# Conditioning rows loaded into the activations' places, a later place for two steps of the first layer's mixers, and another order in the first and last head of the convolution

## The chip, the cores and the metric

The kernel runs on one core of a Trainium2 chip. The metric is the device time of one execution in microseconds (us), and the median of several executions is shown. A core has the engines TensorE (PE, matrix products and transposes), VectorE (DVE), ScalarE (ACT), GpSimd (POOL) and SyncE (SP). Here SP issues the transfers between memory and the core's buffers, one after the other in the order of its queue.

## The reference

A network of two layers works on 1280 tokens (256 of context, then 1024) of width 1024. Each sub-layer is a norm, a modulation by conditioning vectors, a mixer or SwiGLU, and a gated residual.

```
mod = silu(c) @ ada_w + ada_b                    # six vectors for each layer
h   = rmsnorm(x) * (1 + scale) + shift
# layer 0: 4 heads of a bidirectional mLSTM (chunks), and 32 groups of a bidirectional S5:
s_t = a * s_(t-1) + B u_t       (complex)         # the scan
y   = gelu(C s + d * u); b = (y @ wg) glu         # "glu"
x   = x + gate * (concat(norm(mlstm) * sigmoid(o), b) @ w_out)
# layer 1: q, k, v = silu(conv3x3(h @ w_in)), 8 heads of a gated delta rule, both directions
S_t = a_t (I - b_t k_t k_t^T) S_(t-1) + b_t k_t v_t^T;  o_t = S_t^T q_t
x   = x + gate * swiglu(...)                      # after the mixer of each layer
```

## The kernel before

Activations lie with features on the 128 partitions and tokens along the row, in three chunks of 256, 512 and 512 tokens (`CHUNKS`). A dense product splits both operands into a high and a low part and runs three matmuls for each of 8 slices (L124 to L126): `pd` takes 24 matmuls for 128 output features of one chunk, and that is the piece by which the program counts. Each weight block arrives as `w_raw` and is split by ACT (`w_hi`) and POOL (`w_lo`).

The work is written as generators that yield after each piece. `merge`, `take` and `chain` weave them, and the numbers at the head of the file say how many pieces of one go between those of another. PE's order is fixed by that (`in_pe_order`). The other engines are ordered by the framework's scheduler, which looks at a model of the time; marks such as `high_priority` and `issue_after` bind it.

**Entry** (`entry`, `load_x`, `cond_steps`). The tokens come as ten loads `x_raw` of 512 KB (two of context, eight of x), and are transposed to the activations by PE (`x_pt`). Their sums of squares go through a scratch row (`junk`). Two of the six vectors of layer 0, units (0, 0) and (0, 1), are needed for the first norm: their 8 MB come as sixteen `a_raw` loads of 512 KB. `x_raw` and `a_raw` share one ring of three buffers (`self.araw`). PE multiplies the rows with the vectors (`a_ps`), the result is copied to `a_sb`, transposed (`a_pt`), and the norm (`nb_ps`, then tiles `hh` and `hl`, high and low part of the activation) follows. Meanwhile DVE works out the poles of the S5 part (`s5_poles`).

**Layer 0 up to the mixers** (`layer0`). The projection `mlstm_project` has 48 pieces (16 blocks of weights by three chunks). `NI` of them stand in the chain that is merged with `s5_in_matrices` (DVE makes `s_w`, PE transposes it to `s_pb`), `NP` with the products `s_ps` that feed the scan, `NQ` with the matrices of the way out (`s_pk`), `NR` with `mlstm_gates` (`g_pt`), and the rest with the conditioning of the other four vectors. The scan itself runs on DVE, L1080 to L1083, four operations for a step, on the tile `bst`.

**Mixers.** `mlstm_outputs` goes through 12 groups (four heads, each in groups of 4, 4 and 2 chunks of tokens). For each group there are weights (`s_ps`, `e_ps`), heads (`z_ps`; `hsum` is normed by `nv` and `rstd`), and `mlstm_finish` some groups later (`y_pt` transposes `hsum`). The next head's states (`k_pt` and `v_pt` transpose `kT` and `vT`, DVE scales to `kd`, products `c_ps`) are woven in. `N1` of its pieces come alone, then `N2` pieces beside the 16 pieces of `s5_outputs` (`s_py`), then `N3` beside `M2` of `s5_glu`. `s5_outputs` first exchanges two halves of the scan's states by three transfers, each of which needs the one before:

```
with self.tc.issue_after(self.last_load):
    nc.sync.dma_start(out=sw, in_=a)      # L1095 sw_dr<-bst
    nc.sync.dma_start(out=a, in_=b)       # L1096 bst<-bst
    nc.sync.dma_start(out=b, in_=sw)      # L1097 bst<-sw_dr
```

`last_load` is the load of `vT` that was written last in the program (L565). `vT` has one buffer.

**Convolution of layer 1** (`gdn_project`, once for each of 8 heads). The three blocks of k, q and v are projected (`pd`), convolved on DVE (`cv_acc`) and put through a tanh (`d_fT`, `d_qT`). Side work is pulled between the matmuls of a `pd` at the places that the last argument of `conv_block` names, (3, 5) by default. The side work is `gdn_keys`: it transposes k and q to tokens (`tt_ps`), from the sums makes factors (`ei`, on ACT), transposes them (`d_pr`), DVE copies and subtracts (`rows`), and `d_pE` spreads the rows by matmuls. `K0`, `K1`, `Y1`, `Y2`, `L1`, `L2` are numbers of empty yields ahead of these steps. Heads 0 and 7 lay keys and queries in other places than heads 1 to 5, and heads 6 and 7 have no gate block of their own. `set_side` empties the old side work before it puts new work there.

Of the kernel before, what the change touches and what calls it, by code (L numbers as in the profile page):

```python
# [6 lines left out]
F32 = mybir.dt.float32  # L7
# [3 lines left out]
AF = mybir.ActivationFunctionType  # L11
# [16 lines left out]
HP = 400  # L28
Y1, Y2 = 6, 2
K0, K1, K2 = 4, 7, 3  # L30
R0, R1, R2, R3 = 3,1,1,2
F1, F2 = 20,8
L1, L2 = 4,2
F3, F4 = 18, 12
G1, G2, G3 = 2, 2, 14
N1, N2, N3, M2 = 40, 45, 68, 12
W1, W2, NI, NJ, NP, NK, NQ, NR = 1, 2, 2, 2, 4, 2, 10, 8

# [4 lines left out]
class Kernel:  # L43
# [137 lines left out]

    def cond_steps(self, i, m, kk):

# [4 lines left out]
        for k0 in range(0, KB, kk):  # L188
            raw = self.araw.tile([P, kk, D], F32, name="a_raw", tag="a_raw")
            src = w[k0 * P:(k0 + kk) * P, m * D:(m + 1) * D]  # L190
# [6 lines left out]
        sb = self.small.tile([P, 256], F32, name="a_sb", bufs=1)  # L197
        nc.vector.tensor_copy(sb, ps[:, :256])
        yield
# [13 lines left out]

    def cond_many(self, units, kk):
        for i, m in units:
            yield from self.cond_steps(i, m, kk)

# [111 lines left out]
    def load_x(self, hs):  # L329
# [3 lines left out]
        self.ssq = self.const.tile([P, NCH], F32, name="ssq0")  # L333
        junk = hs[2][1].rearrange("p k t -> p (k t)")[:, :D]
        for ci, (t0, n) in enumerate(CHUNKS):
            xt = self.xp.tile([P, KB, n], F32, name=f"x{ci}")
            self.x.append(xt)
            src = self.ins["ctx"][0] if ci == 0 else self.ins["x"][0]
            r0 = 0 if ci == 0 else t0 - NCTX
            for j in range(n // P):  # L340
                raw = self.araw.tile([P, D], F32, name="x_raw", tag="a_raw")
# [99 lines left out]
    def mlstm_gates(self, gk):  # L441
# [81 lines left out]
        self.negm = n1, n2  # L523
        yield
        mt = gp.tile(S, F32, name="g_mt")
        for c0 in range(0, NCH, 8):
# [47 lines left out]
    def mlstm_states(self, h, t, dp, wp):  # L574

        nc = self.nc
        kT, vT = t["kT"], t["vT"]
        vx = t["vx"] = dp.tile([P, NCH, 130], F32, name="vx")
        nc.gpsimd.memset(vx[:, :, 128:130], 1.0)
        kd = [wp.tile([P, NCH, P], F32, name=f"kd{r}") for r in range(2)]  # L580
        for c0, k in ((0, 4), (6, 4), (4, 2)):
# [10 lines left out]
            yield  # L592
        cs = t["cs"] = [dp.tile([P, NCH, 130], F32, name=f"cs{r}") for r in range(2)]
        for i in range(NCH - 1):
# [39 lines left out]
    def mlstm_heads(self, g, t, u, sp):  # L634
# [3 lines left out]
        qT, vx, cs = t["qT"], t["vx"], t["cs"]  # L638
        hsum = u["h"] = sp.tile([P, 4, P], F32, name="hsum", bufs=3)[:, :k]
        zs = [sp.tile([P, 4, 130], F32, name=f"z{r}") for r in range(2)]  # L640
# [25 lines left out]
        ss = sp.tile([P, 4], F32, name="hss")[:, :k]  # L666
        sq = sp.tile([P, P], F32, name="hsq")
        for c in range(k):
            nc.scalar.activation(out=sq, in_=hsum[:, c], func=AF.Square, accum_out=ss[:, c:c + 1])
        rstd = self.norm_rstd(ss, k, 1.0 / P)  # L670
# [17 lines left out]
    def mlstm_outputs(self, dp, wp, sp):  # L688
# [6 lines left out]
        n = len(self.GROUPS)  # L695
        for i in range(n + 3):
            parts = []
# [8 lines left out]
            yield from self.merge(parts)  # L706
            if i > 2:
                g = self.GROUPS[i - 3]
                yield from self.mlstm_finish(g, ts[g[0]], us[i - 3])
            if i < n and i % 3 == 0 and g[0] < 4:  # L710
# [17 lines left out]
    def emit(self, *streams):  # L728

        for _ in self.merge(streams):  # L730
            pass
# [399 lines left out]
    def entry(self, hs, mp, keep, st):  # L1131
# [11 lines left out]
        def emit(gen, n=1000):  # L1143
            for _ in self.take(gen, n):
                pass

        x = self.load_x(hs)
        with ExitStack() as s1:
            cp = self.pool("cp", 1, st=s1)
            self.cond_vectors(cp)  # L1150
            poles = self.s5_poles(keep)
            next(poles)
            emit(x, 2)
            cond = self.cond_many([(0, 0), (0, 1)], 1)
            emit(cond, 2)
            emit(poles)
            emit(cond, 2)
            self.cond_columns(cp)
            emit(self.merge([(cond, 16), (self.take(x, 4), 4)]))
        u_in = self.s5_inputs(hs, mp, self.pool("wu", 1, st=st))  # L1160
        with self.tc.issue_after(self.last_load):
            emit(u_in, 1)
        norm(0)
        norm(1)
# [227 lines left out]
    def layer0(self):  # L1392
# [6 lines left out]
        with ExitStack() as s0:  # L1399
# [4 lines left out]
            self.s5k = self.pool("s5q", 1, st=sk)  # L1404
            hs = [self.acts(ci) for ci in range(3)]
            with ExitStack() as s1:
# [18 lines left out]
            sk.close()  # L1425
            self.emit((self.take(proj, NR), NR), (self.mlstm_gates(mg), 9))
            self.conv_taps()
# [321 lines left out]
    def gdn_project(self, hs, h, tp, qp, kp, bp):  # L1749
# [3 lines left out]
        def start():  # L1753
            self.set_side(self.gdn_keys(h, kqv, kp, qp))
            self.pull()
        kT = tp.tile([P, T], F32, name="d_fT", bufs=3)
        self.conv_block(hs, D + h * P, 8 + h, kT, True, qp, (2, 3, 5, 6) if last else (3, 5))
        kqv[0] = kT
        self.nc.sync.dma_start(out=self.k_dr[h], in_=kT)
        qT = tp.tile([P, NLAT], F32, name="d_qT", bufs=2)  # L1760
        if last:
            start()
        self.conv_block(hs, h * P, h, qT, False, qp)
        kqv[1] = qT
# [15 lines left out]
    def gdn_keys(self, h, kqv, pool, qp):  # L1780

        nc = self.nc
        kT = kqv[0]
        if h == 7:
            for _ in range(L1):
                yield
        NQ = NCH + self.LCH
# [43 lines left out]
        ej = e3[:, 0]  # L1831
        for _ in range(K1 if together else Y1):
            yield
# [566 lines left out]
```

## Time and profile before

| what | before |
|---|---|
| median of 3 executions | 3572.6 us (3568.52 to 3575.85) |
| profiled execution | 3570.8 us |
| its span, first to last instruction | 3568.8 us |
| mean granted clock of PE | 0.967 of full |
| PE busy | 3341.3 us (94%), 18518 instructions |
| DVE busy | 1863.7 us (52%) |
| ACT busy | 1006.6 us (28%) |
| POOL busy | 971.9 us (27%) |

The span is what the trace covers, and the profiled execution has 2.0 us around it. A share over the whole span says little here, since the stages have different limits. Stages of the trace are: entry 0 to 130 us, layer 0 up to the end of the scan 481, mixers to 680, the rest of layer 0 and its SwiGLU to 1844, convolution to 2411, and the recurrence with the rest of layer 1 to 3569.

### The profile page before, as it was taken

The numbers are of one execution on the slowest core, as the hardware profiler recorded it, in microseconds if no ns is written. First come the engines' busy times: TensorE is split into PE (matmuls) and PEld (weight loads), VectorE is DVE, ScalarE is ACT, GpSimd is POOL, SyncE is SP. The second block draws the span as 40 slices with busy tenths as digits, with TensorE's granted clock in tenths as the row PEclk, the third lists the DMA queues.
The fourth block names the chain that finished last, engine by engine and source line by source line (L and its number), as shares of the span: only waits on it lengthen the run. The fifth ranks groups of instructions, "written<-read, shape, count | busy, mean of one in ns | idle before, by whom it ended". The sixth has DMA issues, their size and how long they took to land. (4 is left out here: it accounts for less than half of the span.)

```text
span 3568.8 us, 48262 instructions
## 1 busy us (share of the span) xinstructions
PE 3341.3 (94%) x18518; PEld 2796.5 (78%) x18527; DVE 1863.7 (52%) x4024; ACT 1006.6 (28%) x2409; POOL 971.9 (27%) x843
## 2 busy tenths in 40 slices
PE   5998979899999999999988999888999999999999
PEld 3787768788888888888777877668897788888888
DVE  6749977624433333333467777776654432323234
ACT  3221125422111111111245545543444211111112
POOL 1011123241111111111342382753334122222223
PEclk6999989999999999999999999899999999999999
DMA  7454676331222121121123334356553011111111
GB/s 235 112 172 128 211 197 192 107 127 36 77 83 66 60 83 60 59 71 42 54 69 97 117 119 125 119 139 204 170 167 111 18 54 45 53 45 54 42 53 65
DMA packets 396187, 360.29 MB, mean 101 GB/s; under 512 B 104123, under 2 KB 329115, under 8 KB 395446
## 3 DMA queue, kind: packets, MB, share of 16 engines
q1 hardware_dynamic: 395958, 357.22, 32.4%
q8 instruction: 146, 2.39, 0.3%
q14 instruction: 83, 0.68, 0.1%
HBM read 258.92 MB, written 96.75 MB: 100 GB/s over the span
## 5 line engine op out<-in xcount | busy, mean ns | idle before, releaser
L124 PE MATMUL pd<-hh,w_hi 128*128 128x512 f32 (+1 forms) x3064 | 1158.2, 378 | 3.0 <-ACT hh L289 2.0
L126 PE MATMUL pd<-hh,w_lo 128*128 128x512 f32 (+1 forms) x3064 | 1134.6, 371 | 5.6 <-POOL w_lo L118 5.2
L125 PE MATMUL pd<-hl,w_hi 128*128 128x512 f32 (+1 forms) x3064 | 1137.5, 371 | 2.4 <-DVE hl L281 2.2
L118 POOL TENSOR_TENSOR w_lo<-w_raw,w_hi 128x1024 fp32r<-128x1024 f32 (+2 forms) x205 | 479.8, 2341 | 2001.5 <-ACT w_hi L117 1977.3
L124 PEld LDWEIGHTS pd<-hh,w_hi 128*128 128x128 f32 x3064 | 587.1, 192 | 118.4 <-issue 6.0
L126 PEld LDWEIGHTS pd<-hh,w_lo 128*128 128x128 f32 x3064 | 585.8, 191 | 111.4 <-POOL w_lo L118 9.3
L125 PEld LDWEIGHTS pd<-hl,w_hi 128*128 128x128 f32 x3064 | 586.8, 192 | 102.4 <-DVE hl L281 5.3
L117 ACT CAST w_hi<-w_raw 128x1024 fp32r<-128x1024 f32 (+2 forms) x205 | 207.4, 1012 | 927.1 <-PE pd L125 695.2
L1344 DVE SCALAR_TENSOR_TENSOR x<-pd,mod,x 128x512 f32<-128x512 f32 (+1 forms) x408 | 265.6, 669 | 226.1 <-PE pd L126 226.1
L124 PE MATMUL pd<-g_hi,w_hi 128*128 128x512 f32 (+1 forms) x844 | 307.8, 365 | 0.0
L125 PE MATMUL pd<-g_lo,w_hi 128*128 128x512 f32 (+1 forms) x844 | 306.9, 364 | 0.0
L126 PE MATMUL pd<-g_hi,w_lo 128*128 128x512 f32 (+1 forms) x844 | 304.1, 363 | 0.6 <-POOL w_lo L118 0.6
L1703 DVE SCALAR_TENSOR_TENSOR cv_acc<-img,wcv,cv_acc 128x512 f32<-128x512 f32 x384 | 279.6, 751 | 40.0 <-ACT img L1674 24.9
L1332 DVE TENSOR_TENSOR ntmp<-ntmp,pd 128x512 f32<-128x512 f32 (+1 forms) x110 | 69.8, 634 | 416.0 <-PE pd L126 415.6
L1331 DVE SCALAR_TENSOR_TENSOR ntmp<-ntmp,pd 128x512 f32<-128x512 f32 (+1 forms) x110 | 69.7, 634 | 380.8 <-ACT ntmp L1330 380.8
L124 PEld LDWEIGHTS pd<-g_hi,w_hi 128*128 128x128 f32 x844 | 159.2, 189 | 27.9 <-ACT w_hi L117 2.5
L126 PEld LDWEIGHTS pd<-g_hi,w_lo 128*128 128x128 f32 x844 | 158.9, 188 | 26.4 <-POOL w_lo L118 1.0
L125 PEld LDWEIGHTS pd<-g_lo,w_hi 128*128 128x128 f32 x844 | 159.2, 189 | 24.5
L1334 DVE SCALAR_TENSOR_TENSOR g_lo<-ntmp,g_hi 128x512 fp32r<-128x512 f32 (+1 forms) x110 | 139.8, 1270 | 64.1 <-ACT g_hi L1333 64.1
L1333 ACT ACTIVATE g_hi<-ntmp 128x512 fp32r<-128x512 f32 (+1 forms) x110 | 64.7, 588 | 349.2 <-DVE ntmp L1332 348.9
L1330 ACT ACTIVATE ntmp<-pd 128x512 f32<-128x512 f32 (+1 forms) x110 | 60.7, 552 | 247.9 <-PE pd L126 247.9
L250 POOL TENSOR_TENSOR nacc<-nacc,ntmp 128x256 f32<-128x256 f32 (+1 forms) x72 | 74.2, 1035 | 125.5 <-ACT ntmp L246 124.0
(544 smaller groups left out, 4531.4 us busy)
## 6 DMA issues: line engine op xcount, KB each, us to landing
w_raw<-in_ffn_w_dram SPq DMA_DIRECT2D x106, 512.0 KB
a_raw<-in_ada_w_dram SPq DMA_DIRECT2D x40, 1024.0 KB
w_raw<-in_od_w_in_dram SPq DMA_DIRECT2D x32, 512.0 KB
w_raw<-in_ffn_w_dram SPq DMA_DIRECT2D x32, 384.0 KB
w_raw<-in_ev_w_in_dram SPq DMA_DIRECT2D x20, 512.0 KB
a_raw<-in_ada_w_dram SPq DMA_DIRECT2D x16, 512.0 KB
x_dr<-x SPq DMA_DIRECT2D x4, 2048.0 KB
p_dr<-mp_t SPq DMA_DIRECT2D x32, 256.0 KB
```

The costliest lines, as they stand in the source:

```text
L117: nc.scalar.copy(out=hi, in_=raw)
L118: self.w_lo_engine.tensor_tensor(out=lo, in0=raw, in1=hi.bitcast(F32), op=ALU.subtract)
L124: mm(ps, lh, rh, start=first, stop=False)
L125: mm(ps, lh, rl, start=False, stop=False)
L126: mm(ps, ll, rh, start=False, stop=last)
L250: nc.gpsimd.tensor_tensor(out=acc, in0=acc, in1=sq, op=ALU.add)
L1331: nc.vector.scalar_tensor_tensor(out=th[:, :n], in0=th[:, :n], scalar=1.0, in1=p1, op0=ALU.add, op1=ALU.mult)
L1332: nc.vector.tensor_tensor(out=th[:, :n], in0=th[:, :n], in1=p3, op=ALU.mult)
L1333: nc.scalar.activation(out=gh[:, t0:t0 + n], in_=th[:, :n], func=AF.Copy, scale=0.5)
L1334: nc.vector.scalar_tensor_tensor(out=gl[:, t0:t0 + n], in0=th[:, :n], scalar=0.5, in1=gh[:, t0:t0 + n].bitcast(F32), op0=ALU.mult, op1=ALU ...
L1344: nc.vector.scalar_tensor_tensor(out=xd, in0=ps, scalar=g, in1=xd, op0=ALU.mult, op1=ALU.add)
L1703: nc.vector.scalar_tensor_tensor(out=a, in0=src, scalar=wc(i), in1=a, op0=ALU.mult, op1=ALU.add)
```

## The change

The conditioning rows of the two vectors come as eight loads of 1 MB, each straight into a part of an activation tile of chunk 1 or 2 that is not in use yet (`places`), and these tiles are given to the activations afterwards. The ring of three serves the tokens alone there. The scratch row is taken from another tile. The copy `a_sb` is done by ACT and no longer by DVE, for all units. The numbers `NI`, `NR`, `N1`, `N3`, `Y1`, `Y2`, `K0`, `G1` and `G2` change, `mlstm_gates` has one yield more, and `mlstm_finish` comes four groups behind and no longer three, with a fourth buffer for `hsum` (the memory comes from narrower `vx` and `cs`, and from `hsq`, which `z` replaces). In the last head of the convolution the keys' work is strung behind the side work that is there, which is not emptied first, the wait `L1` goes, and the places at which side work is pulled move from the k block to the q block. In head 0 `d_pr` has two yields more ahead of it.

```diff
@@ -26,15 +26,15 @@
-Y1, Y2 = 6, 2
-K0, K1, K2 = 4, 7, 3
+Y1, Y2 = 8, 4
+K0, K1, K2 = 6, 7, 3
...
-L1, L2 = 4,2
+L2 = 2
...
-G1, G2, G3 = 2, 2, 14
-N1, N2, N3, M2 = 40, 45, 68, 12
-W1, W2, NI, NJ, NP, NK, NQ, NR = 1, 2, 2, 2, 4, 2, 10, 8
+G1, G2, G3 = 3, 3, 14
+N1, N2, N3, M2 = 58, 45, 50, 12
+W1, W2, NI, NJ, NP, NK, NQ, NR = 1, 2, 4, 2, 4, 2, 10, 9
@@ -179,14 +179,14 @@
-    def cond_steps(self, i, m, kk):
+    def cond_steps(self, i, m, kk, places=None):
...
-            raw = self.araw.tile([P, kk, D], F32, name="a_raw", tag="a_raw")
+            raw = next(places) if places else self.araw.tile([P, kk, D], F32, name="a_raw", tag="a_raw")
...
-        nc.vector.tensor_copy(sb, ps[:, :256])
+        nc.scalar.copy(out=sb, in_=ps[:, :256])
@@ -331,12 +331,12 @@
-        junk = hs[2][1].rearrange("p k t -> p (k t)")[:, :D]
...
+            junk = hs[2 if ci == 2 else 0][1].rearrange("p k t -> p (k t)")[:, :D]
@@ -522,6 +522,7 @@
         self.negm = n1, n2
         yield
+        yield
@@ -575,8 +576,8 @@
-        vx = t["vx"] = dp.tile([P, NCH, 130], F32, name="vx")
+        vx = t["vx"] = dp.tile([P, NCH, 129], F32, name="vx")
...
-        cs = t["cs"] = [dp.tile([P, NCH, 130], F32, name=f"cs{r}") for r in range(2)]
+        cs = t["cs"] = [dp.tile([P, NCH, 129], F32, name=f"cs{r}") for r in range(2)]
@@ -636,7 +637,7 @@
-        hsum = u["h"] = sp.tile([P, 4, P], F32, name="hsum", bufs=3)[:, :k]
+        hsum = u["h"] = sp.tile([P, 4, P], F32, name="hsum", bufs=4)[:, :k]
@@ -664,9 +665,8 @@
-        sq = sp.tile([P, P], F32, name="hsq")
         for c in range(k):
-            nc.scalar.activation(out=sq, in_=hsum[:, c], func=AF.Square, accum_out=ss[:, c:c + 1])
+            nc.scalar.activation(out=zs[0][:, c, 0:P], in_=hsum[:, c], func=AF.Square, accum_out=ss[:, c:c + 1])
@@ -693,7 +693,7 @@
-        for i in range(n + 3):
+        for i in range(n + 4):
...
-            if i > 2:
-                g = self.GROUPS[i - 3]
-                yield from self.mlstm_finish(g, ts[g[0]], us[i - 3])
+            if i > 3:
+                g = self.GROUPS[i - 4]
+                yield from self.mlstm_finish(g, ts[g[0]], us[i - 4])
@@ -1151,15 +1151,19 @@
             next(poles)
             emit(x, 2)
-            cond = self.cond_many([(0, 0), (0, 1)], 1)
-            emit(cond, 2)
+
+            flat = [h.bitcast(F32).rearrange("p k t -> p (k t)") for ci in (1, 2) for h in self.acts(ci)]
+            places = iter([f[:, o:o + 2 * D].rearrange("p (k n) -> p k n", n=D) for f in flat for o in (0, 2 * D)])
+            cond = self.cond_many([(0, 0), (0, 1)], 2, places)
+            emit(cond, 1)
             emit(poles)
-            emit(cond, 2)
             self.cond_columns(cp)
-            emit(self.merge([(cond, 16), (self.take(x, 4), 4)]))
+            emit(cond, 5)
+            emit(self.merge([(cond, 6), (self.take(x, 4), 4)]))
...
+        hs.extend(self.acts(ci) for ci in (1, 2))
@@ -1402,7 +1406,7 @@
-            hs = [self.acts(ci) for ci in range(3)]
+            hs = [self.acts(0)]
@@ -1423,7 +1427,7 @@
-            self.emit((self.take(proj, NR), NR), (self.mlstm_gates(mg), 9))
+            self.emit((self.take(proj, NR), NR), (self.mlstm_gates(mg), 10))
@@ -1751,16 +1755,20 @@
         def start():
-            self.set_side(self.gdn_keys(h, kqv, kp, qp))
-            self.pull()
+            keys = self.gdn_keys(h, kqv, kp, qp)
+            if last:
+                self.side = self.chain(self.side, keys)
+            else:
+                self.set_side(keys)
+                self.pull()
...
-        self.conv_block(hs, D + h * P, 8 + h, kT, True, qp, (2, 3, 5, 6) if last else (3, 5))
+        self.conv_block(hs, D + h * P, 8 + h, kT, True, qp)
...
-        self.conv_block(hs, h * P, h, qT, False, qp)
+        self.conv_block(hs, h * P, h, qT, False, qp, (2, 4, 6) if last else (3, 5))
@@ -1781,9 +1789,6 @@
-        if h == 7:
-            for _ in range(L1):
-                yield
@@ -1829,7 +1834,7 @@
-        for _ in range(K1 if together else Y1):
+        for _ in range((K1 + 2 * (h == 0)) if together else Y1):
             yield
```

The queue of SP at the start of the program, from the second load of conditioning rows (`in_ada_w_dram`; the first stands three rows ahead) through those of the tokens (`x_raw`, all of x here), before:

```order
L191 DMA a_raw<-in_ada_w_dram 128x1024
L434 DMA g_bias<-in_ev_f_bias_dram 4x1
L191 DMA a_raw<-in_ada_w_dram 128x1024 x3
L342 DMA x_raw<-in_x_dram 128x1024
L191 DMA a_raw<-in_ada_w_dram 128x1024 x2
L342 DMA x_raw<-in_x_dram 128x1024
L191 DMA a_raw<-in_ada_w_dram 128x1024 x4
L342 DMA x_raw<-in_x_dram 128x1024
L191 DMA a_raw<-in_ada_w_dram 128x1024 x4
L342 DMA x_raw<-in_x_dram 128x1024
L113 DMA w_raw<-in_ev_w_in_dram 128x8x128 x2
```

and of the change, from the first load of conditioning rows on, which now go to tiles named `hh` and `hl`:

```order
L191 DMA hh_195<-in_ada_w_dram 128x2x1024
L191 DMA hl_196<-in_ada_w_dram 128x2x1024 x2
L191 DMA hh_197<-in_ada_w_dram 128x2x1024
L342 DMA x_raw<-in_x_dram 128x1024
L191 DMA hh_197<-in_ada_w_dram 128x2x1024
L342 DMA x_raw<-in_x_dram 128x1024
L191 DMA hl_198<-in_ada_w_dram 128x2x1024 x2
L342 DMA x_raw<-in_x_dram 128x1024
L434 DMA g_bias<-in_ev_i_bias_dram 4x1 x2
L434 DMA g_bias<-in_ev_f_bias_dram 4x1 x2
L342 DMA x_raw<-in_x_dram 128x1024
L113 DMA w_raw<-in_ev_w_in_dram 128x8x128 x2
```

Eight loads of 1 MB stand for sixteen of 512 KB, five of them ahead of the first load of x; the order of the token loads among themselves is the same.

SP's queue around the exchange of the scan's states, before. The first four rows load head 1, the row of vT behind `s_w` loads head 2:

```order
L566 DMA vT<-p_dr 128x1280
L566 DMA kT<-p_dr 128x1280
L566 DMA qT<-p_dr 128x1280
L566 DMA so<-p_dr 128x1280
L1095 DMA sw_dr<-bst 64x5184
L1041 DMA s_uu<-u_dr 128x4x160
L1103 DMA s_t_5192<-tt_dr 128x4x128
L1106 DMA s_w_5194<-wc_dr 64x4x256 x2
L1041 DMA s_uu<-u_dr 128x4x160
L1103 DMA s_t_5313<-tt_dr 128x4x128
L1106 DMA s_w_5315<-wc_dr 64x4x256 x2
L566 DMA vT<-p_dr 128x1280
```

and of the change, from the same loads of head 1 (kT, qT, so) on:

```order
L567 DMA kT<-p_dr 128x1280
L567 DMA qT<-p_dr 128x1280
L567 DMA so<-p_dr 128x1280
L567 DMA vT<-p_dr 128x1280
L1095 DMA sw_dr<-bst 64x5184
L1041 DMA s_uu<-u_dr 128x4x160
L1103 DMA s_t_5406<-tt_dr 128x4x128
L1106 DMA s_w_5408<-wc_dr 64x4x256 x2
L1041 DMA s_uu<-u_dr 128x4x160
L1103 DMA s_t_5510<-tt_dr 128x4x128
L1106 DMA s_w_5512<-wc_dr 64x4x256 x2
L567 DMA kT<-p_dr 128x1280
```

The load of head 2's vT has moved from behind the mixing weights `s_w` to a place just ahead of `sw_dr<-bst`, and its kT now stands ahead of `bst<-bst`.

PE in head 6 of the convolution, from `d_pr` (the transposed factors) to the first `d_pE`, before:

```order
L1837 MATMUL d_pr<-ident,ei_0_15410 128x128
L124 MATMUL pd<-hh_14630,w_hi 128x256
L125 MATMUL pd<-hl_14631,w_hi 128x256
L126 MATMUL pd<-hh_14630,w_lo 128x256
L124 MATMUL pd<-hh_14630,w_hi 128x256
L125 MATMUL pd<-hl_14631,w_hi 128x256
L126 MATMUL pd<-hh_14630,w_lo 128x256
L124 MATMUL pd<-hh_14630,w_hi 128x256
L125 MATMUL pd<-hl_14631,w_hi 128x256
L126 MATMUL pd<-hh_14630,w_lo 128x256
L1859 LDWEIGHTS sel_15336
L1859 MATMUL d_pE<-rows_0_15406,sel_15336 128x128
```

and of the change, the last rows ahead of the first `d_pE`; `d_pr` stands 27 rows ahead of the first of them, and all the rows between are matmuls of `pd` with 512 columns:

```order
L124 MATMUL pd<-hh_15016,w_hi 128x512
L125 MATMUL pd<-hl_15017,w_hi 128x512
L126 MATMUL pd<-hh_15016,w_lo 128x512
L124 MATMUL pd<-hh_15016,w_hi 128x512
L125 MATMUL pd<-hl_15017,w_hi 128x512
L126 MATMUL pd<-hh_15016,w_lo 128x512
L1864 LDWEIGHTS sel_15304
L1864 MATMUL d_pE<-rows_0_15374,sel_15304 128x128
```

Before, nine matmuls of 256 columns lie between the two; in the change 33 of 512 columns do. In heads 1 to 5 the 15 matmuls of 512 columns have become 33 as well.

## Rows read from the trace of the kernel before

**Rows 1.** Stretches: us, busy of PE PEld DVE ACT POOL, PEclk, DMA share, GB/s

```profile
0.00:100.00 100.00, 61.64 (x333) 40.75 (x334) 66.88 (x234) 36.21 (x62) 16.59 (x49) 0.71 0.67 217
130.00:182.00 52.00, 43.09 (x222) 36.47 (x221) 48.53 (x51) 12.91 (x22) 5.24 (x2) 0.90 0.35 105
235.00:481.00 246.00, 228.02 (x1443) 180.31 (x1442) 230.44 (x756) 40.76 (x65) 41.67 (x21) 0.97 0.53 170
481.00:530.00 49.00, 31.46 (x207) 27.55 (x210) 29.44 (x100) 15.90 (x60) 12.85 (x12) 0.79 0.88 219
600.00:640.00 40.00, 28.96 (x191) 23.30 (x192) 37.43 (x127) 23.23 (x84) 18.75 (x17) 0.87 0.35 103
1844.00:2411.00 567.00, 497.73 (x2735) 413.11 (x2733) 433.96 (x775) 278.42 (x806) 283.91 (x359) 0.94 0.38 117
```

**Rows 2.** Waits of PE, 0 to 100 us: us in total, times, longest

```profile
PE a_ps L194 <- DMA a_raw<-in_ada_w_dram: 13.4, 11, 2.6
```

**Rows 3.** Two stretches, columns as in rows 1, for the transfers

```profile
40.00:50.00 10.00, 6.03 (x40) 2.10 (x39) 4.05 (x18) 1.45 (x3) 0.00 (x0) 0.50 0.85 264
475.00:480.00 5.00, 2.68 (x21) 2.10 (x19) 4.72 (x12) 2.72 (x4) 2.52 (x3) 1.00 0.99 342
```

**Rows 4.** Timeline of PE near 51 us: start, us, instruction, [idle before <- releaser]

```profile
51.09 1.94 PE L349 MATMUL x_pt<-ident,x_raw 128*128 128x128 f32 x8 [2.21 <-DMA x_raw<-in_x_dram]
```

**Rows 5.** Waits of PE, 130 to 182 us

```profile
PE s_pb L961 <- DVE s_w L944: 8.9, 5, 3.2
```

**Rows 6.** Groups of DVE, 235 to 481 us: busy us, mean ns

```profile
L198 DVE COPY a_sb<-a_ps 128x256 f32<-128x256 f32 x4 | 1.7, 417 | 0.0
```

**Rows 7.** Waits of PE, 235 to 481 us

```profile
PE a_pt L202 <- DVE a_sb L198: 4.7, 2, 2.4
```

**Rows 8.** Timeline of SP's issues, 480 to 530 us

```profile
485.63 0.50 SPq L1095 DMA_DIRECT2D sw_dr<-bst  x1
...
501.09 0.52 SPq L1096 DMA_DIRECT2D bst<-bst  x1
...
518.84 0.47 SPq L1097 DMA_DIRECT2D bst<-sw_dr  x1
```

**Rows 9.** Timeline of PE in the same stretch, heads 0 and 1

```profile
498.47 0.38 PE L590 MATMUL v_pt<-ident,vT 128*128 128x128 f32 x2
...
505.54 0.39 PE L648 MATMUL z_ps<-cs,qT 128*128 128x129 f32 x2
505.76 0.39 PE L649 MATMUL z_ps<-vx,e_sb 128*128 128x129 f32 x2
```

**Rows 10.** Waits of PE, 481 to 680 us

```profile
PE s_py L1114 <- issue: 8.0, 1, 8.0
PE y_pt L680 <- DVE nv L223: 7.7, 1, 7.7
PE s_py L1114 <- DMA bst<-sw_dr: 6.9, 1, 6.9
PE y_pt L680 <- DVE hsum L671: 5.3, 1, 5.3
```

**Rows 11.** Waits of PE, 1844 to 2411 us

```profile
PE d_pE L1859 <- DVE rows L1841: 18.6, 6, 7.7
PE d_pr L1837 <- ACT ei L1805: 16.8, 4, 7.3
```

**Rows 12.** Timeline of PE in the convolution: head 0, and d_pE of head 1

```profile
1892.85 0.39 PE L125 MATMUL pd<-hl,w_hi 128*128 128x512 f32 x1
1893.08 0.39 PE L126 MATMUL pd<-hh,w_lo 128*128 128x512 f32 x1
1899.66 0.47 PE L1837 MATMUL d_pr<-ident,ei 128*128 128x128 f32 x1 [6.20 <-ACT ei L1805]
...
1961.73 0.61 PE L1859 MATMUL d_pE<-rows,sel 128*128 128x128 bf16 x8 [1.90 <-DVE rows L1841]
```

**Rows 13.** A stretch behind the d_pr of head 0, columns as in rows 1

```profile
1900.00:1905.00 5.00, 5.00 (x13) 3.90 (x13) 4.73 (x10) 0.56 (x1) 0.00 (x0) 0.50 0.00 0
```

More of the change, by code (lines that the diff above doesn't have):

```diff
@@ L212, in cond_steps, with cond_many @@
         yield
-    def cond_many(self, units, kk):
+    def cond_many(self, units, kk, places=None):
         for i, m in units:
-            yield from self.cond_steps(i, m, kk)
+            yield from self.cond_steps(i, m, kk, places)
     def norm_rstd(self, ssum_cols, n, scale=1.0 / D):
@@ L577, in mlstm_states @@
         kT, vT = t["kT"], t["vT"]
-        vx = t["vx"] = dp.tile([P, NCH, 130], F32, name="vx")
-        nc.gpsimd.memset(vx[:, :, 128:130], 1.0)
+        vx = t["vx"] = dp.tile([P, NCH, 129], F32, name="vx")
+        nc.gpsimd.memset(vx[:, :, 128:129], 1.0)
         kd = [wp.tile([P, NCH, P], F32, name=f"kd{r}") for r in range(2)]
```

## The prediction

> **What bounds the kernel now.** I read the table of stretches first. TensorE (PE) is busy for most of every stretch, so the question for each is what fills the rest [rows 1]. In 0 to 100 us it is data: PE works 61.6 of 100 us. In 130 to 182 and in 235 to 481 it is VectorE (DVE), busy 48.5 of 52 and 230.4 of 246 us: PE has work left over there, and DVE's last result sets the end. In 481 to 530 PE works 31.5 of 49 us, while the DMA engines are 88% busy. In 600 to 640 DVE is busy 37.4 of 40 us. In the convolution stage, 1844 to 2411, PE works 497.7 of 567 us and DVE only 434.0: PE is the bound and loses time in single waits. The lists of waits then say which ones, and single instructions where they lie.
>
> **1. Entry.** PE waits 13.4 us in 11 places for conditioning rows a_raw [rows 2]. The reader should see why the rows are late: they share a ring of three buffers with the tokens x_raw, so SyncE cannot issue the next load until PE has read an old buffer. Hence 40 to 50 us still moves only 264 GB/s at share 0.85, though a stretch with enough transfers queued moves 342 at share 0.99 [rows 3]. The fourth token load of chunk 1 (call it x4), behind which the program goes on to the first norm, is transposed at 51.09, after a wait for its transfer [rows 4].
> The change gives each of the eight conditioning loads (1 MB each) a place of its own. What must have landed by x4 is the context (1.05 MB, which I take to be there by 8 us: 5 us at the 217 GB/s of the whole stretch, behind some 3 of start), 8.39 MB of rows and 2.1 MB of tokens. These 10.5 MB at 320 to 342 GB/s take 31 to 33 us, so x4 lands at 39 to 41. From 51.1 that is 10 to 12 us earlier. Three token buffers still wait for PE, and DVE has the 66.9 us of this stretch in an unchanged order, so I keep **8 us** (5 to 11). Behind it PE and DVE have a chain without slack up to 182 us, so it carries.
> The Trainium skill, "DMA: Bandwidth & Descriptors", section "Bandwidth", gives 341 GB/s for a 1 MB transfer and asks for transfers of that size. The 342 above agrees; by the page's figure alone (an estimate) x4 would land at about 38.5 and the term be 12.
>
> **2. Layer 0 up to the mixers.** In 130 to 182 PE waits 8.9 us for s_w [rows 5], and two more projection pieces (NI) fill that. It buys nothing: between the s_pb of DVE's last s_w and the last s_ps ahead of the scan both orders have four pieces of 512 columns and two of 256. In 235 to 481 DVE runs the scan, and the first kd of the mixers stands behind the whole scan on DVE in both orders. So PE's waits inside, such as 4.7 us for a_sb [rows 7], and the longer cover by NR, are worth nothing; only the four a_sb copies, 1.7 us, leave DVE [rows 6]. **1 us**, from -2 (the weight of the extra pieces is converted on GpSimd beside DVE's s_w) to 4.
>
> **3. Mixers.** Two terms. First the exchange of the scan's states: three chained transfers, sw_dr<-bst at 485.63, bst<-bst at 501.09, bst<-sw_dr at 518.84 [rows 8], for which s_py waits 8.0 and 6.9 us [rows 10]. Count from T = 481, where the scan ends; the last part is used at 528, T+47. N1 = 58 puts 18 more head pieces ahead of s_py. They hold 24 z_ps, 8 s_ps and 4 c_ps, which start 0.22 us apart [rows 9], 20 transposes, which as single passes I put at half of that, and 9 e_ps of about the same 0.22: 7.9 + 2.2 + 2.0, 12 us of PE work. Before, these pieces came behind the exchange and were done 12 us after T+47, at T+59 but for other waits; now they are done while it runs, so the gain is T+59 - L, where L is when the exchange lands now. But L moves: the exchange is issued behind the last load of vT, which is now head 2's, and that waits for the last v_pt of head 1, at 498.47 [rows 9]. So it starts at T+17.5 and no longer at T+4.5. Its three steps took 15.5, 17.7 and 9.2 us. The first two ran beside head 1's loads, now finished; the third ran alone. If they go as before, L = T+60 and nothing is gained; if all go like the third, T+45, a gain of 14. I take 11+12+9 = 32, L = T+50: **9 us** (-1 to 14).
> Second, y_pt waits 7.7 us for nv and 5.3 us at the end for hsum [rows 10]. It now comes a group later. In 600 to 640 DVE itself is full, so most of the first wait only moves: 3. Of the second, whose cover grows by 24 matmuls of 320 columns (3.5 us), 3. **6 us** (3 to 9).
>
> **4. Convolution.** Two waits dominate: d_pE for rows, 18.6 us in 6, and d_pr for ei, 16.8 in 4 [rows 11]. A 512-column pd follows the one before it after 0.23 us at full clock [rows 12], one of 256 after half of that; between d_pr and d_pE stood 15 of them, now stand 33, 4.1 us more. The 1.90 of a middle head [rows 12] has three equals, so four heads give 7.6. The d_pE of head 3 (18.6 - 4 x 1.9 - 7.7 = 3.3) is covered too: 3.3. In head 6 nine matmuls of 256 columns (1.1 us) become 33 of 512 (7.6): 6.4 of its 7.7, the longest [rows 11]. In head 0 d_pr comes 30 pd later, 6.8 us, against 6.20 [rows 12]: 6.2. In head 7, where the keys' work is strung behind the side work rather than put ahead of it, d_pr comes 27 pd later, 6.1 of 7.3, the longest of its kind [rows 11]. Sum 29.6. DVE's queue moves little (rows of head 0 and of head 7 stand 2 to 3 us of DVE work later), and I take off 2 for a new short wait of d_pE in head 7.
> After such a wait PE is slow as well: in the 5 us behind the 6.20 the granted clock is 0.50, that is 1.2 GHz, and 13 instructions run where full clock does 22 [rows 13]. That is some 2 us for each of the long waits in heads 0, 6 and 7 and less in head 3; I add 1.5, since other waits remain ahead of the same places. **29 us** (16 to 38; the low end if each newly covered result meets a next one that DVE delivers late: half of the middle, with no clock regained).
>
> The recurrence of layer 1 and the dense stages have the same order in both kernels: 0.
>
> **Sum.** 8 + 1 + 9 + 6 + 29 = 53. The profiled execution took 3570.8 us, so 3518; the median of the runs shown is 1.8 higher, hence **3520**.
>
> **Rivals.**
> *PE's waits count everywhere* (more gain). If the scan were held back by what PE feeds, the 4.7 us of a_pt and the 8.9 of s_pb would be worth their time as well: 14 more, about 3506. Against it: DVE's 230.4 of 246 [rows 1]. 6%.
> *The exchange gains nothing.* Its transfers run into head 2's kT, qT and the mixing weights just as before into head 1's, L = T+59: 9 less, 3529; with the entry at its low end as well 3533. I count this inside the forecast's range.
> *Convolution held by DVE.* The results that were late (rows, ei, d_qT) come from DVE and ACT in high priority; if PE, freed, only meets the next of them, a third of the 29 stays: 10, so 3539. For it: DVE works 434 of 567, and in 1900 to 1905, where PE has just been waiting, it is at 4.73 of 5 [rows 13]. Against it: four middle heads show the single 1.9 us wait and then run on. 20%.
> *The change does not do what it says*: the entry is set by DVE's poles and not by the loads, and rival three holds too: 3570.8 - (1 + 1 + 5 + 6) = 3558, or nearer to no change. 8%, half of it within 0.2% (7 us, about what a measurement of this kernel can tell from no change).
> *Slower: the exchange late by its new place.* SyncE works in order. Head 2's vT now holds up everything behind it, the exchange and then head 2's kT, and all of head 2's k_pt wait for that kT. If sw_dr comes only after T+30 (v_pt late because kd of head 1 stands behind other DVE work), L passes T+75, 16 us lost and PE at half clock behind it, and the groups behind, DVE-full in 600 to 640, lose the 6 as well. This decides only if L is above T+59 by more than the rest gains, 44 us, with the full convolution term; with that at 10 and the entry at 5, by more than 16, at L = T+75. For it: the order of the queue. Against: v_pt at 498.47 does not hang on the changed part. 5%.
>
> **How the numbers follow.** Forecast 61%: 3505 to 3535. The range takes in the convolution rival's 3539 and, below, entry 11, layer 0 at 4, mixers 23 and convolution 32, a sum of 70, 3502; the bad ends together (5 - 2 + 2 + 16 = 21) give 3552. So **3500 to 3552**. Faster by over 0.2%: 61 + 6 + 20 + 4 = 91%; within: 4%; slower: 5%.
>
> **What the new profile would show.** Entry: hardly a wait of a_ps for its rows, share above 0.9 in 20 to 40 us, x4 at 39 to 41 (wrong if above 46). Layer 0: from the first scan step to the first kd still about 246 us; s_pb's waits gone without gain. Mixers: sw_dr issued 17 us after the scan's end and s_py waiting 10 us or less in all. Convolution: the 1.9 us waits gone, d_pr of head 0 and 7 below 2 us, PE's clock 0.97 or more in 1844 to 2411. The prediction is wrong above all if d_pE or tt_ps take up waits of 3 us or more in their place, or if the exchange lands after T+59.

## The result, and the profile after

The changed kernel takes 3532.0 us (median of 4, 3525.5 to 3537.2) where the kernel before takes 3570.6 (median of 4, 3566.5 to 3575.9): a ratio of 0.9889, 95% interval 0.9874 to 0.9903, or 39.6 us less (35 to 45). Forecast were 3520 and a range of 3500 to 3552. The time lies in the range, 12 us above the middle: the convolution's term was 15 us too high, the mixers' terms 5 too high and the entry's 7 too low. Two of the eight executions of e10 below were slow (5456 and 6558 us) and do not count in its time.

The profiled execution has a span of 3535.5 us, 33.3 less than before. The table of stretches of the changed kernel, with the columns of rows 1 and the stretches moved to where the same work now lies (entry; to the end of the scan; 49 us behind it; convolution up to the first `e_pu`):

```profile
0.00:100.00 100.00, 70.74 (x404) 51.57 (x405) 72.21 (x241) 40.54 (x69) 18.16 (x50) 0.85 0.80 240
217.50:463.50 246.00, 222.04 (x1432) 176.47 (x1428) 229.28 (x755) 42.20 (x73) 37.64 (x21) 0.95 0.53 168
463.50:512.50 49.00, 34.52 (x236) 29.69 (x240) 32.33 (x106) 19.62 (x74) 17.19 (x18) 0.81 0.81 187
1824.80:2373.30 548.50, 485.55 (x2722) 404.19 (x2720) 432.84 (x775) 275.03 (x805) 284.04 (x359) 0.96 0.40 121
```

The same convolution work as in the last row, from 1847.2 to 2411.4 in the kernel before:

```profile
1847.20:2411.40 564.20, 494.53 (x2721) 410.50 (x2720) 433.96 (x775) 278.03 (x805) 283.91 (x359) 0.94 0.39 118
```

In the entry PE works 70.7 of 100 us and no longer 61.6, its clock is 0.85 and no longer 0.71, and the transfers' share is 0.80 instead of 0.67 [rows 1]. Around the scan DVE is as full as before. In the convolution stage 15.7 us are gone. PE's idle time there fell from 69.7 to 63.0, so 6.7 of them are waits; 9.0 are PE's own busy time, with one instruction more, at a granted clock of 0.96 for 0.94. The profiles of e2 and e9 below, with the same work in that stage, have 61.0 and 62.0 us idle and 486.9 and 484.4 busy.

Followed along the program (differences of start times between the two traces): the fourth token load of chunk 1 is transposed 13.6 us earlier, the scan begins 13.4 and ends 17.4 us earlier, the first piece behind the mixers stands 22.2 earlier, the convolution starts 22.4 and ends 38.1 earlier, and the end of the span is 33.3 earlier. The last 4.8 were lost in the recurrence, whose order did not change. In a second profile of the changed kernel (e9 below) that loss is 1.5, and the stage from the scan's end to the convolution took 4 us less. A stage of unchanged code differs by 3 us and more from one profile to another, so stage differences of that size are not read here.

The waits of PE in the mixers, 463 to 650 us, of the changed kernel (us in total, times, longest), which answer to [rows 10]:

```profile
PE k_pt L585 <- DMA kT<-p_dr: 11.3, 1, 11.3
PE k_pt L585 <- DVE kd L587: 10.1, 1, 10.1
PE z_ps L649 <- DVE z L653: 7.5, 4, 4.1
PE s_py L1114 <- DMA bst<-sw_dr: 3.3, 1, 3.3
```

The 13.0 us of `y_pt` are gone, and of the 14.9 us of `s_py` 3.3 are left. In their place stand 11.3 us for head 2's kT and 10.1 for kd (3.6 before), which stands behind the scan on DVE. The longer wait for kd goes with the small parts of layer 0: it is 3.2 us with the entry alone (e1), 3.8 with the mixers alone (e3) and 3.7 with these parts undone (e8).

And in the convolution, 1820 to 2380 us, which answer to [rows 11]:

```profile
PE tt_ps L1722 <- DVE d_qT L1710: 11.6, 3, 5.5
PE d_pe L1876 <- ACT d_e L1881: 10.2, 5, 3.0
PE tt_ps L1722 <- ACT tt_sq L1730: 7.0, 5, 2.4
PE d_pr L1842 <- ACT ei L1810: 6.3, 3, 2.9
PE d_pe L1876 <- ACT d_qE L1866: 5.9, 5, 1.2
...
PE d_pE L1864 <- DVE rows L1846: 2.4, 3, 0.9
```

`d_pE` fell from 18.6 to 2.4 and `d_pr` from 16.8 to 6.3, as foreseen. But `d_pe`, the next products of the same chain, now wait 16.1 us for ACT where they waited 3.6 for `d_e`.

### The profile page after: what moved, and what is told of

It is laid out like the page before. It is cut to its first block, busy times and chain, and to the rows that moved or that the text cites. A ratio compares the mean times of both kernels' runs of the same rounds, so it can differ in the third digit from the quotient of the medians.

```text
span 3535.5 us, 48232 instructions
## 1 busy us (share of the span) xinstructions
PE 3321.6 (94%) x18519; PEld 2784.6 (79%) x18527; DVE 1860.5 (53%) x4012; ACT 1003.7 (28%) x2421; POOL 967.7 (27%) x843
## 4 chain that ended last, share of the span: by engine, by line
PE 39%; DVE 7%; ACT 2%; DMA 2%; issue 1%; SPq 1%; POOL 0%; DVEq 0%; POOLq 0%; ACTq 0%
PE pd L124 10%; PE pd L125 10%; PE pd L126 10%; DVE cv_acc L1707 2%; PE e_pk L2094 1%; PE e_pu L2102 1%; PE e_ps L2125 1%; PE e_acc L2116 1%; PE e_pp L2027 1%; PE e_pw L2015 1%; PE e_acc L2120 1%; ACT tt_sq L1730 1%; DMA e_vt<-v_dr 0%; DVE hl L281 0%; DVE b_x L1947 0%
## 5 line engine op out<-in xcount | busy, mean ns | idle before, releaser
L1336 DVE TENSOR_TENSOR ntmp<-ntmp,pd 128x512 f32<-128x512 f32 (+1 forms) x110 | 69.7, 634 | 416.3 <-PE pd L126 416.1
L1335 DVE SCALAR_TENSOR_TENSOR ntmp<-ntmp,pd 128x512 f32<-128x512 f32 (+1 forms) x110 | 69.7, 633 | 380.8 <-ACT ntmp L1334 380.8
```

Source lines behind the costliest of these rows:

```text
L1335: nc.vector.scalar_tensor_tensor(out=th[:, :n], in0=th[:, :n], scalar=1.0, in1=p1, op0=ALU.add, op1=ALU.mult)
L1336: nc.vector.tensor_tensor(out=th[:, :n], in0=th[:, :n], in1=p3, op=ALU.mult)
```

## The experiments

Each was timed against the kernel before on the same chip, in three groups of four kernels. Differences are worked out from the ratio; the intervals are 95%.

**Entry alone** (e1), the kernel before with

```diff
-            cond = self.cond_many([(0, 0), (0, 1)], 1)
-            emit(cond, 2)
+            cond = self.cond_many([(0, 0), (0, 1)], 2, places)
+            emit(cond, 1)
```

and what hangs on it (places, `hs`, `junk`, order of `emit`).

> The kernel before with the entry part of the change alone (rows in the activations' places, loads of 1 MB; a_sb stays on DVE, all numbers and the rest as before). Theory A, the entry gives what the trace of the changed kernel shows at the scan's first step (226.4 against 239.8) and nothing behind it gives that back: the first step of the scan 13 us earlier, the scan itself as long as before (241 us), time 13 us less, about 3557. Rival B, the entry is worth the 8 us of my prediction and the rest of the 13.4 came from the pieces of NI ahead of the scan: first step 8 us earlier, 3562. Rival C, what is won is taken back in the mixers, whose waits are for transfers: 3565 or more.

Measured: ratio 0.9958 (0.9946 to 0.9971), 15 us less (10 to 19). The scan's operation L1083 (duration ns min/median/max, first and last start), in the kernel before:

```profile
L1083 DVE TENSOR_TENSOR bst<-s_t,bst x159: 261/282/2484, 239.8 to 480.9; 128x64 f32<-128x64 f32 x159
```

in the changed kernel:

```profile
L1083 DVE TENSOR_TENSOR bst<-s_t,bst x159: 271/282/2482, 226.4 to 463.5; 128x64 f32<-128x64 f32 x159
```

and with the entry alone:

```profile
L1083 DVE TENSOR_TENSOR bst<-s_t,bst x159: 269/282/2481, 223.0 to 463.9; 128x64 f32<-128x64 f32 x159
```

With the entry alone the scan begins 16.8 us earlier and keeps its length. In the changed kernel it begins 3.4 later than that and is 4 us shorter. The length goes with the small parts of layer 0 (240.8 us in e8 and 240.5 in e12, which undo them). The later start is not explained: with NI back at 2 it begins at 224.0 in e8 but at 227.0 in e12. The entry carries through, as A says, and is larger than both A and B put it at the scan. The run changes the size of the loads, their places and the order of the pieces at once; it does not tell these apart.

**Convolution alone** (e2), the kernel before with all edits of `gdn_project` and `gdn_keys` and the numbers Y1, Y2, K0, L1, G1, G2.

> The kernel before with the convolution part of the change alone (Y1, Y2, K0, K1+2 of head 0, L1, G1, G2, last head's side work). Theory A, as in the trace of the changed kernel: 16 us won between the first gate product and the first e_pu, and 4 to 5 us given back behind it in the recurrence, whose first waits grow: 11 us less, about 3559. Rival B, the loss behind it belongs to something else in the change: 16 us less, 3554. Rival C, the 29 us of my prediction were there and the earlier parts spoiled them: 3541.

Measured: 0.9962 (0.9948 to 0.9975), 13.6 us less (9 to 19). The stage from `dg_ps` to `e_pu` takes 547.9 us, as in the changed kernel, and its heads have the same lengths within 1.3 us. Behind it 1.2 us are given back, so B is nearer than A; C falls: the missing half of the 29 was never there.

**Mixers alone** (e3), the kernel before with N1, N3, the later `mlstm_finish` and its buffers.

> The kernel before with the mixers part alone (N1 = 58, N3 = 50, mlstm_finish a group later, four buffers of hsum, narrower vx and cs). Theory A, the exchange of the scan's states, now behind head 2's vT, lands at T+61 as in the changed kernel, so N1 gives nothing and the later finish all: 4 to 5 us less, 3566. Rival B, the 11 us wait for head 2's kT and the late exchange appear only because the earlier parts bring PE there too early: then 10 to 15 us less, 3558. Rival C, both together cost more than the finish gives: no change or slower, 3570 to 3575.

Measured: 0.9973 (0.9964 to 0.9982), 9.6 us less (6 to 13). The exchange is issued at 497.7 and its last step at 529.0, with the scan's last step at 479.1; head 2's `k_pt` wait 9.6 us for kT here as well, so these waits do not come from the earlier parts. The gain lies between A and B; C falls.

**N1 and N3 back** (e4), the changed kernel with

```diff
-N1, N2, N3, M2 = 58, 45, 50, 12
+N1, N2, N3, M2 = 40, 45, 68, 12
```

> The changed kernel with N1 and N3 back at 40 and 68, all else as changed. The exchange is issued ahead of head 2's vT again. Theory A, N1 was worth nothing or cost up to 2 us, since the exchange moved by as much as it hid: 3530 to 3533, the same as the changed kernel or slightly faster, exchange landing at T+47 and s_py waiting some 15 us. Rival B, the pieces in front are worth the larger part of what the mixers won: 3536 to 3540.

Measured: 0.9903 (0.9889 to 0.9917), against 0.9889 and 0.9891 of the changed kernel: some 5 us slower, with intervals that overlap. The exchange is issued 4.8 us behind the scan's end again and `s_py` waits 11.9 us in two. `y_pt` waits 6.4 us for `hsum` again, so N1 and N3 have a share in that term too. B is favoured, not shown.

**Exchange in two steps** (e5), the changed kernel with

```diff
             nc.sync.dma_start(out=sw, in_=a)
-            nc.sync.dma_start(out=a, in_=b)
+            nc.sync.dma_start(out=sw2, in_=b)
+            nc.sync.dma_start(out=a, in_=sw2)
             nc.sync.dma_start(out=b, in_=sw)
```

> The changed kernel, with the exchange of the scan's states in two steps that run side by side inside (both halves to memory, then both back), where it was a chain of three. Theory A, the transfers hold the mixers: the states land at T+45 and not T+61, head 2's kT is not behind a third step, the waits of k_pt (11.3 us) and s_py (3.3 us) shrink to 5 together, and 5 to 10 us are won: 3522 to 3527. Rival B, the mixers end with VectorE and ScalarE anyway (in the changed kernel PE is 4 us ahead of the kernel before at its last s_py and 20 ahead at its last y_pt): the waits for transfers shrink and waits of z_ps for z grow, 0 to 2 us won: 3529 to 3532.

Measured: 0.9895 (0.9881 to 0.9909), nothing won. `s_py` has no wait for `bst` left in its list, but head 2's kT was issued at 500.2 and no longer at 494.5, since the loads ahead of it in the queue took longer to issue behind two transfers of the states (18.5 us from the first transfer's issue to kT's, 13.2 in the changed kernel), and `k_pt` waits for it 14.1 us. What one transfer gained the next one lost. B has the time right; its cause (waits of z_ps growing) is not what the list shows: those for z are 6.0, where the changed kernel has 7.5.

**Y2 alone** (e6): `Y1, Y2 = 6, 2` becomes `6, 4` in the kernel before.

> The kernel before with Y2 = 4 alone, which gives d_pE the longer cover in all heads. My prediction's terms: 7.6 for four middle heads, 3.3 for head 3 and 6.4 for head 6, 17 us less, 3553. Theory A, from the traces of the changed kernel and of the convolution part alone: in the middle heads the wait only moves on to the next link (d_pe for ScalarE's d_qE, 1.2 us in each, and d_pe for d_e, 3.0 in head 3), so these give 3 to 4 us, and head 6 gives its 5 to 6: 9 us less, 3561. Rival, head 6 as well meets its next link: 4 us less, 3566.

Measured: 1.0010 (1.0001 to 1.0019), 3.6 us slower (0.4 to 7). All expectations fall. In its trace the middle heads, from head 1's `d_pr` to head 6's, take 324.9 us for 327.1, the same as in the changed kernel; from head 6's `d_pr` to `e_pu` 128.1 us became 132.7.

**Last head alone** (e7): `self.chain(self.side, keys)` in place of `set_side`, Y1 = 8, no L1, the moved pulls, G1 and G2, in the kernel before.

> The kernel before with what the change does in the last head of the convolution alone (keys' work strung behind the side work, Y1 = 8, no L1, pulls moved from the k block to the q block, G1 and G2 = 3). My prediction's term: 4 to 6 us less, 3564 to 3566. Theory A, from the intervals between the d_pr of heads 6 and 7 (69.7 us before, 56.5 with the convolution part alone, of which 4 to 6 are only the later place of d_pr): the last head and the end of head 6's side work give 7 to 9 us: 3561 to 3563.

Measured: 0.9996 (0.9988 to 1.0005), no change. The prediction's term and Theory A fall.

**Y2 and last head together** (e10), nothing else.

> The kernel before with Y2 = 4 and the last head's part together, which alone gave +3.6 and -0.6 us; head 0 stays as before. Theory A, the two need each other: the last head no longer empties head 6's side work, so that head 6's d_pE gets the 33 pieces of cover that Y2 asks for, and the last head's d_pE has the cover that the later d_pr uses up; then d_pE of head 6 waits about 1 us (9.6 and 6.4 with one part alone), d_pr of the last head about 1 (9.0 and 5.9), and the time is 11 to 13 us less, 3557 to 3559. Rival B, what the convolution part won lies in head 0, whose part neither run had: 0 to 3 us less, 3567 or more.

Measured: 0.9973 (0.9962 to 0.9984), 9.6 us less (6 to 14). The two edits that gave nothing alone give most of the convolution's gain together. The timeline of PE shows why. Head 6's `d_pE` and the last head's `d_pr`, with Y2 alone:

```profile
2287.96 1.01 PE L1859 MATMUL d_pE<-rows,sel 128*128 128x128 bf16 x8 [9.59 <-DVE rows L1841]
...
2349.14 0.48 PE L1837 MATMUL d_pr<-ident,ei 128*128 128x128 f32 x1 [9.02 <-ACT ei L1805]
```

with the last head alone:

```profile
2296.97 1.01 PE L1860 MATMUL d_pE<-rows,sel 128*128 128x128 bf16 x8 [6.36 <-DVE rows L1842]
...
2347.16 0.47 PE L1838 MATMUL d_pr<-ident,ei 128*128 128x128 f32 x1 [5.88 <-ACT ei L1806]
```

and with both:

```profile
2294.27 1.01 PE L1860 MATMUL d_pE<-rows,sel 128*128 128x128 bf16 x8 [3.77 <-DVE rows L1842]
...
2340.31 0.33 PE L1838 MATMUL d_pr<-ident,ei 128*128 128x128 f32 x1 [0.98 <-ACT ei L1806]
```

With Y2 alone the last head's `set_side` still empties head 6's side work in one go, so the two more yields bring no matmuls and `d_pE` waits as before: nine matmuls of 256 columns stand between head 6's `d_pr` and it, as in the kernel before. With the chain alone the yields are there, but too few: 15 matmuls of 512 columns. With both there are 33. Head 6's wait is at 3.8 and not at 1 in e10. In e2, which has head 0's part too, it is 1.0, but in e4, with the same convolution, 2.1; what sets it is open.

**Head 0 alone** (e11): K0 = 6 and `K1 + 2 * (h == 0)` in the kernel before.

> The kernel before with head 0's part alone (K0 = 6, two yields more ahead of d_pr). My prediction's term: 6 to 8 us less, 3562 to 3564. Theory A, from the traces: d_pr of head 0 comes 6.8 us of PE work later, but its wait of 6.2 is then spent in tt_ps for DVE's d_qT and in the keys' tail, so 1 to 2 us less, 3568. Rival B, the parts of the other heads needed it: nothing or slower here, 3570 to 3574.

Measured: 0.9994 (0.9985 to 1.0003), 2 us less, not told from nothing. In its profile the stretch from `dg_ps` to head 1's `d_pr` is 5.2 us shorter than before, but PE's idle time in it is 16.6 us for 17.6. The rest is PE's busy time, 87.2 for 91.4, at a granted clock of 0.97 up to head 0's `d_pr` and 1.00 behind it, for 0.89 and 0.95. The two parts e10 and e11 add up to 11.7, near e2's 13.6.

**Small parts of layer 0 undone** (e8), the changed kernel with NI = 2, NR = 8, nine yields of the gates and `a_sb` on DVE.

> The changed kernel with the small parts of layer 0 undone: NI, NR and the yields of the gates as before, a_sb copied by VectorE again; entry, mixers and convolution as changed. Theory A, these parts are worth nothing together: the scan begins 3 us earlier than in the changed kernel (226.4 there, 223.0 with the entry alone) and lasts 3 to 4 us longer (237 there, 241 with the entry alone): time the same within 2 us, 3530 to 3534. Rival B, PE's waits in this stretch count: 5 us or more slower, 3537.

Measured: 0.9874 (0.9859 to 0.9889), 3525.6 us. The scan runs from 224.0 to 464.8, as A says, and B falls, but the time is 4 us below A's.

**The changed kernel again** (e9).

> The changed kernel itself once more, beside the three others on the same chip, so that small differences to it can be told. Both theories on the layer-0 parts need its time here: 3532 as in its first runs. If it comes at 3526 here, the 6 us by which the kernel with those parts undone was faster were scatter between runs.

Measured: 0.9891 (0.9876 to 0.9906), 3529.9 us. So e8 stands 4 to 6 us ahead of it, which two intervals of this width do not separate.

**Both candidates** (e12): e8 with the exchange in two steps.

> The changed kernel with the small parts of layer 0 undone and the exchange of the scan's states in two steps, the candidate for a version faster than both. Theory A, the first of the two is worth 5 us and the second nothing, as in their own runs (the wait of s_py goes, the wait of k_pt for head 2's kT grows, since that load now runs beside both transfers of the first step): 3524 to 3527. Rival B, the two together let PE run on: 3520 or less. Rival C, the 5 us were scatter: 3530 to 3533.

Measured: 0.9902 (0.9888 to 0.9915), 3535.2 us, slower than e8 by 10 us. `k_pt` waits 17.0 us in two for kT here, which is 9 more than in e8. But the transfer does not explain the 10 us. Of the 14.7 us between the profiles of e8 and e12 2.8 lie ahead of the scan's end, 2.2 between it and the convolution, and 9.7 behind, where the code is the same. The time is nearest to C, and a second pair speaks for C as well: e12 is e5 with the layer-0 parts undone, and takes 3535.2 us against 3532.1. Undoing them comes out 4 to 6 us faster in one pair and 2 to 3 slower in the other. No version was shown to be faster than the changed kernel.

## Why the prediction was right, and where its terms were not

The time fell inside the range and inside the forecast's 3505 to 3535, but partly by luck: in the convolution what happened is what the rival "Convolution held by DVE" priced at 10 us, not the forecast's 29, and an entry 7 us better than forecast made up for part of it. Of the signs that the prediction named against itself, one came in full and one in part: the exchange landed after T+59, and waits of up to 3.0 us came up at the next link, at `d_pe` where `d_pE` and `tt_ps` were named (`tt_ps` waits up to 5.5 us, but it waited 4.1 before). PE's clock in the convolution is 0.96 and not 0.97. The signs for the transfers' share in the entry (1.04 in 20 to 40 us) and for `s_py` came true; of the waits of `a_ps` for its rows 7.4 of 13.4 us are left.

- **Entry, 8 us forecast, 15 measured alone.** The mechanism was right; the size failed at the transfer rate. I took 342 GB/s as what a full queue moves [rows 3], from a stretch in which loads of 640 KB ran. With its loads of 1 MB queued the changed kernel moves more, by its table of stretches:

```profile
20.00:30.00 10.00, 8.18 (x67) 3.59 (x59) 5.92 (x42) 2.48 (x5) 0.00 (x0) 0.53 1.03 412
```

  so x4 is transposed at 37.5 us and not at 39 to 41. Then I took 2 to 4 us off for DVE. PE does wait for DVE right behind (7.3 us of `nb_ps` for `ntmp`, 5.7 before), but these waits are 10.7 us in all where they were 10.6, and the stage kept all of the gain. The chunk-1 norm at 72.6 for 88.6 shows 2.4 more; PE's higher clock in the entry would do that, which no run isolates. The 341 GB/s that the Trainium skill, "DMA: Bandwidth & Descriptors", section "Bandwidth", gives for a transfer of 1 MB stand in its table of transfers issued from GpSimd. The 412 GB/s of the loads queued here on SP exceed them.
- **Layer 0, 1 us forecast.** Undoing these parts made the kernel no slower (e8). That PE's waits beside the scan are worth nothing holds: in the changed kernel PE stands 10.1 us waiting for kd right behind it, in e8 3.7. The rival in which they count falls. From the scan's first step (L1083) to the first kd it is 241.3 us before and 237.3 after; the 246 of the prediction counts from 235 us, 5 us ahead of that step. So that stretch of DVE is 4 us shorter, where I had counted 1.7; but the scan begins 2.4 us later than in e8 and ends only 1.3 earlier.
- **Mixers, 9 + 6 forecast, 9.6 measured alone.** The exchange was issued 17.8 us behind the scan's end (17.5 forecast) and its last part used at T+60.8. That is the bound "as before" and not the T+50 that I took. SP's timeline (start, us, instruction):

```profile
481.32 0.50 SPq L1095 DMA_DIRECT2D sw_dr<-bst  x1
...
494.48 1.61 SPq L567 DMA_DIRECT2D kT<-p_dr  x1
496.13 0.51 SPq L1096 DMA_DIRECT2D bst<-bst  x1
...
514.59 0.47 SPq L1097 DMA_DIRECT2D bst<-sw_dr  x1
```

  Its steps took 14.8, 18.5 and 9.7 us. I had freed them of head 1's loads but not counted head 2's, which now run beside them. Nor was it right that both steps had run beside head 1's loads before: beside the second, issued at 501.09 [rows 8], ran head 2's vT and kT, as SP's timeline of the kernel before shows:

```profile
500.03 1.02 SPq L566 DMA_DIRECT2D vT<-p_dr  x1
...
505.28 0.33 SPq L566 DMA_DIRECT2D kT<-p_dr  x1
```

  In the changed kernel the load of kT needs from 494.5 to 509.3, and PE waits for it, by its timeline:

```profile
509.26 1.12 PE L585 MATMUL k_pt<-ident,kT 128*128 128x128 f32 x4 [11.29 <-DMA kT<-p_dr]
...
524.28 0.90 PE L1114 MATMUL s_py<-bst,s_w 128*128 128x160 f32 x2 [3.31 <-DMA bst<-sw_dr]
```

  So the exchange's 9 is the step that failed, by its own formula to -2. The wait of `y_pt` went altogether, 13.0 us, where I had counted 6, but `z_ps` waits 7.5 us for z where it waited 0.6. How the 9.6 are shared between N1 and the later finish stays open: e4 gives N1 some 5, not resolved.
- **Convolution, 29 us forecast, 13.6 measured alone.** The stage in three parts, up to head 1's `d_pr`, from there to head 6's, and from there to `e_pu` (columns as in rows 1), before:

```profile
1847.18:1956.14 108.96, 91.38 (x484) 75.39 (x483) 89.33 (x168) 55.31 (x167) 41.70 (x37) 0.92 0.28 92
1956.14:2283.27 327.13, 303.95 (x1680) 252.70 (x1679) 258.86 (x453) 168.34 (x494) 160.64 (x221) 0.96 0.39 120
2283.27:2411.40 128.13, 99.22 (x559) 82.42 (x560) 85.78 (x156) 54.38 (x146) 81.57 (x102) 0.89 0.47 136
```

  and in the changed kernel:

```profile
1824.78:1932.41 107.63, 91.87 (x485) 76.38 (x483) 85.73 (x168) 55.15 (x167) 41.54 (x37) 0.92 0.28 93
1932.41:2257.29 324.88, 300.60 (x1689) 250.60 (x1688) 259.86 (x455) 168.97 (x497) 155.50 (x211) 0.97 0.39 121
2257.29:2373.27 115.98, 93.07 (x553) 77.19 (x551) 87.25 (x154) 50.91 (x142) 87.00 (x113) 0.96 0.52 150
```

  For heads 6 and 7 the size came out, 12.1 won where 10.5 were forecast, and only by the two edits together, which I had priced one by one. It came out partly by luck. The waits of `d_pE` for `rows` and of `d_pr` for `ei` there did fall from 15.0 to 3.4 us, but those of `d_pe` and `d_pk` for ACT rose from 1.4 to 10.0, and PE's idle time fell by only 6.0. Of the other 6.1, 1.1 come from head 6's `d_pr` standing nine matmuls of 256 columns later, and the rest is busy time at a clock of 0.96 for 0.89. The step that failed is the middle heads' 7.6 + 3.3: 327.1 us became 324.9 (323.8 without the nine matmuls), and PE's idle time rose from 23.2 to 24.3. The wait for `rows` is gone, but the next link of the chain waits instead, here in head 1 of the changed kernel's timeline:

```profile
1946.14 0.27 PE L1876 MATMUL d_pe<-maskb,identb 128*128 128x256 bf16 x1 [1.22 <-ACT d_qE L1866]
```

  Heads 1, 2, 4 and 5 have this 1.2, and heads 3 and 6 a wait of 3.0 for `d_e`. The rival "Convolution held by DVE" was right in kind: PE, freed, meets the next result. The engine of the new waits is ACT and not DVE. Head 0's 6.2 failed alike: its `d_pr` waits no more, but between it and head 1's `d_pr` stand 6.0 us of waits for ACT (`d_pe`, `tt_ps`) where 0.9 stood, and the stage up to head 1's `d_pr` is 1.3 us shorter. PE's busy time, for whose clock I had added 1.5, gave 9.0 of the 15.7 us. So of the 27.6 us of waits that I had summed 6.7 went.

The sum of the parts timed alone, 15 + 9.6 + 13.6 = 38, is near the whole change's 39.6: no disturbance of one by another shows, within intervals of some 4 us for each.

## What to carry to other kernels

A wait that gets more cover is worth its length only if nothing later in the same chain is late; price the chain up to its end, not the link. Two edits can each be worth nothing and need one another (yields that a drain discards, a drain that has no yields to keep), so edits of one mechanism are tried together before one is dropped. When a transfer is moved, list what it will run beside at the new place, since its price is that of the company.

## What the runs showed of the hardware that was not expected

Loads of 1 MB, queued on SP ahead of their use, moved 412 GB/s in 20 to 30 us together with the token loads, where I had taken the 342 of [rows 3] for the most. The load of head 2's kT (640 KB) took 14.8 us to its first use, beside one more of 640 KB (qT) and a transfer of 1296 KB between two halves of the partitions, and that transfer took 18.5 us. More than half of a stage's gain was PE's busy time: in the convolution it fell from 494.5 to 485.6 us with 2722 instructions for 2721, while the idle time fell from 69.7 to 63.0 and the granted clock rose from 0.94 to 0.96.
